# mLSTM projections as pairs in block products, with h as scratch, and the SWA groups and mLSTM heads in steps

## The chip, the cores and the metric

One core of one Trainium2 chip. The time is the device time of one execution in microseconds; a kernel's time is the median of its runs. Profiles come from one execution with the hardware profiler.

## The reference

Two layers on a residual stream h of 256 rows and 2048 columns, all in float32:

- Layer 0: RMSNorm, one input projection, then sliding-window attention (16 query heads of 64 in 4 groups, each group with one key and value head, window 128, ALiBi, a sink per head) beside an mLSTM with 4 heads (q and k of 128, v of 256, an output gate o, an input and a forget gate per head, chunks of 128 rows). Both results are joined and go through one output projection, which is added to h.
- Layer 1: RMSNorm, forgetting attention with 16 heads of 128, output projection, added to h.
- Behind each mixer: RMSNorm and a SwiGLU with 5632 hidden columns, added to h. At the end a last RMSNorm.

The change lies in the mixer of layer 0:

```python
proj = xn @ w_in
q_s, k_s, v_s, q_m, k_m, v_m, o_m, i_m, f_m = split_cols(proj, EVEN_SIZES)
attn = sliding_window_attention(q_s, k_s, v_s, sinks)
h = mlstm_chunkwise(q_m, k_m, v_m, i_pre, f_pre)
h = rms_norm(h, head_gain)
mem = sigmoid(o_m) * h
return concat([attn, mem]) @ w_out
```

## The kernel before

Every float32 matmul against weights is done as three float32r matmuls of 128 x 128 by 128 x 512: each operand is split into a high and a low part, and high by high, high by low and low by high are added in PSUM. Weights come in chunks of two k tiles by 512 columns (`load_raw`, on SyncE's DMA queue, four buffers). ScalarE rounds a chunk to `hi` (L153), VectorE subtracts to get `lo` (L154); `hi` and `lo` have six buffers. `gemm` (L167) runs a range of k tiles for both row tiles t: L181 to L183. `project` (L192) is a `gemm` over all 16 k tiles, 96 matmuls for 512 columns. x, transposed and split, lies in `xh` and `xl`; the mixer's result in `mh` and `ml`.

`pair_group` (L408) makes two projections of one x at once, for gate and up of the SwiGLU, for its down projection, and for q and k of layer 1. It goes through the eight pairs of k tiles in a given order. A plain pair costs 24 matmuls. In three of the eight pairs the two row tiles, two k tiles and two matrices are combined as in a fast matrix product: seven block products of three matmuls in place of eight, 21 matmuls. For it VectorE forms four differences of weight blocks (L439, L440, L444, L445), both engines split them (`split_plain`, L255 and L256), and beforehand the sums and differences of x are made for that pair (`sums_of`, `sums_from`). The products of the three pairs add up in four PSUM banks `prods`; at the end VectorE combines them into four tiles `c` (L464 to L468), and the plain part is added to them.

`Room` hands `pair_group` its buffers: the second matrix's raw chunks, `t4`, `c` and `tmp` from a pool, and the places for split differences, either from a pool or, in layer 1, in the free halves of `mh` and `ml`.

PSUM has two sets of four banks: `pa` (accumulators, tag acc) and `pm` (everything else: transposes `pp`, `ptm`, `ptv`, scores `p0`, `p1`, P times V `po`, gates `pu`, `pn`, `pb`, the heads' `pc` and `pom`).

Layer 0's mixer in the order of the code: keys and values of SWA (acc0), the first half of the SWA queries (acc1), while h is loaded and its squares are summed (L616, ScalarE); groups 0 and 1 of SWA; the second half of the queries; groups 2 and 3 (`swa`, `attention`); the tail of the output gate with the eight gate columns (264 columns); the chain of the gates: `pu`, two scans on VectorE (L725 to L733), `pn` (L739, L740), `pb` (L763), the decay matrix `dt_`; the rest of the output gate (512 and 256 columns, `gate_out`); q, its transposes; k, its transposes; q times k (`pq`); then, for each half of the value columns, a projection and two heads (`mlstm`). Then `close_layer` does the output projection (`out_proj`, L350) and the SwiGLU.

The order in which an engine runs its instructions is not that of the code: the framework lays it out when the kernel is built, by a timeline of its own, and puts ready matmuls of later projections into earlier gaps. Each engine runs its list in order. In the built order of the kernel before, the SWA groups stand among the matmuls of the output gate and of q, the heads among those of the values and of the output projection.

A head (L820) is: `pc`, copied to `ce`; per chunk of 128 rows `pom`, its denominator (ScalarE L832, VectorE L833, L836), `hv` (L837), its squares (ScalarE L839); a small power on GpSimd (L841); `hv` times the gate (L843); four transposes `ptv` (L854); split into `mh` and `ml`.

Of the kernel before, what the change touches and what calls it, by code (L numbers as in the profile page):

```python
# [7 lines left out]
F32 = mybir.dt.float32  # L8
# [34 lines left out]
V_AT = 8  # L43
MID = 6
# [12 lines left out]
def trunk(  # L57
# [158 lines left out]
    def sums_of(pool, sh, sl, copies, full=None):  # L216
        if full is None:
            full = pool.tile([P, 2, NT, P], F32, tag="tmp", name="full", bufs=2)
            copies(full.rearrange("p i t q -> p i (t q)"))
        s = pool.tile([P, 4, P], F32, tag="tmp", name="s4", bufs=2)  # L220
# [177 lines left out]

    def sums_from(room, sh, sl, lhs, pair):
# [6 lines left out]
        sums_of(room.pool, sh, sl, None, full)  # L406
# [64 lines left out]
    def ffn(layer, fp, sx, sd, key, idx_next=None, key_next=None, finish=None):  # L471
# [7 lines left out]
        for g0, g1 in zip(PARTS, PARTS[1:]):  # L479
# [4 lines left out]
            for g in range(g0, g1):  # L484
# [15 lines left out]
                if g == g1 - 1 and nk < 16:  # L500
                    for half in range(2):
                        pt = bank(par, "pf").rearrange("p (i q) -> p i q", i=2)
                        for i in range(2):
                            cs = (2 * half + i) * P
                            for t in range(NT):
                                nc.tensor.transpose(pt[:, i, t * P : (t + 1) * P], c[:, t, cs : cs + P], ident)
                        pair = 2 * (g - g0) + half
                        k = 2 * pair
                        split_plain(mh[:, k : k + 2, :], ml[:, k : k + 2, :], pt)
                        if pair in mixed_of(order):  # L510
                            j = mixed_of(order).index(pair)
                            sums_of(
                                fp, sd[0][:, j, :, :], sd[1][:, j, :, :], lambda full, pt=pt: nc.scalar.copy(full, pt)
                            )
                    continue
# [7 lines left out]
                def join(c=c, turned=turned, g=g, g0=g0, order=order):  # L523
# [8 lines left out]
                    for half in range(2):  # L532
                        pair = 2 * (g - g0) + half
                        if pair in mixed_of(order):
                            j = mixed_of(order).index(pair)
                            sums_of(
                                fp,
                                sd[0][:, j, :, :],
                                sd[1][:, j, :, :],
                                None,  # L540
                                ct[:, half * 512 : (half + 1) * 512].rearrange("p (i t q) -> p i t q", i=2, t=NT),
                            )
# [50 lines left out]
    def close_layer(layer, w_out, idx, key, begun=None, **rest):  # L593
        with tc.tile_pool(name=f"fp{layer}", bufs=2) as fp:
            nd = max(len(mixed_of(o)) for o in DOWN.values())
            sd = [fp.tile([P, nd, 4, P], F32R, name=f"sd{i}", bufs=1) for i in range(2)]
            out_proj(w_out, idx, key, (*sx, fp), begun)
            ffn(layer, fp, sx, sd, key, **rest)


# [17 lines left out]
    with tc.tile_pool(name="ev", bufs=1) as ev:  # L618
# [22 lines left out]
        with tc.tile_pool(name="sw", bufs=1) as sw:  # L641
# [17 lines left out]
            def swa(g, qn):  # L659
# [17 lines left out]
                for _ in attention(  # L677
# [10 lines left out]
                ):  # L688
# [15 lines left out]
        acc = project(wi, OFF_OM + 768, 256 + 8)  # L704
# [5 lines left out]
        gate_out(acc, 768, 256)  # L710
        nc.scalar.activation(gates, gates, AF.Tanh, scale=1.0 / CAP)
# [46 lines left out]
        with tc.tile_pool(name="mp", bufs=1) as mp:  # L758
            dt_ = mp.tile([P, ML_H, NT, P], F32, name="dt_")
# [18 lines left out]
            gate_out(project(wi, OFF_OM, NB), 0, NB)  # L778
            gate_out(project(wi, OFF_OM + NB, 256), NB, 256)
# [3 lines left out]
            qm = natural(mp, project(wi, OFF_QM, NB), NB, "qm", scale=rq)  # L783
# [7 lines left out]
            for g in range(0, ML_H, 2):  # L791
                transpose_many(
                    qmt[:, g : g + 2, :].rearrange("p g (t q) -> p (g t) q", q=P),
                    [qm[:, t, (g + i) * QK : (g + i + 1) * QK] for i in range(2) for t in range(NT)],
                )
            transpose_many(qst, [qsc[:, hh, :] for hh in range(ML_H)])
            km = natural(mp, project(wi, OFF_KM, NB), NB, "km")
            kmt = mp.tile([P, ML_H, S], F32, name="kmt")
            for g in range(0, ML_H, 2):
                transpose_many(  # L800
                    kmt[:, g : g + 2, :].rearrange("p g (t q) -> p (g t) q", q=P),
                    [km[:, t, (g + i) * QK : (g + i + 1) * QK] for i in range(2) for t in range(NT)],
                )
            kw = mp.tile([P, ML_H, QK], F32, name="kw")
            for hh in range(ML_H):
                nc.vector.tensor_scalar(
                    kw[:, hh, :], km[:, 0, hh * QK : (hh + 1) * QK], ex[:, 3, hh : hh + 1], None, op0=ALU.mult
                )
            for c in range(NT):
                pq = pm.tile([P, ML_H, P], F32, tag="pm", name="pq")  # L810
# [3 lines left out]
                nc.vector.tensor_tensor(out=dt_[:, :, c, :], in0=pq, in1=dt_[:, :, c, :], op=ALU.mult)  # L814

# [4 lines left out]
            def mlstm(hh):  # L820
                pc = pm.tile([P, NB], F32, tag="pm", name="pc")
                nc.tensor.matmul(pc[:, 0 : VD + 1], kw[:, hh, :], ve[:, 0, hh, :], start=True, stop=True)
                nc.vector.tensor_copy(ce[:, hh, :], pc[:, 0 : VD + 1])
                hv = mp.tile([P, NT, VD], F32, tag="hv", name="hv", bufs=2)
# [17 lines left out]
                for c in range(NT):  # L842
# [7 lines left out]
                    )  # L850
                pt = pm.tile([P, 2, S], F32, tag="pm", name="ptv")
# [6 lines left out]
            for g in range(2):  # L858
                acc = project(wi, OFF_VM + g * NB, NB)
                for t in range(NT):  # L860
                    nc.scalar.mul(
                        ve[:, t, 2 * g : 2 * g + 2, 0:VD],
                        acc[t].rearrange("p (h e) -> p h e", e=VD),
                        r[:, t : t + 1],
                    )
                mlstm(2 * g)
                mlstm(2 * g + 1)
# [3 lines left out]
    close_layer(0, w_out_even[0], 2, "f0", idx_next=1, key_next="m1")  # L871
# [4 lines left out]
    with tc.tile_pool(name="od", bufs=1) as od:  # L876
# [10 lines left out]
        for t in range(NT):  # L887
# [15 lines left out]
        halves = [  # L903
            [m[:, k : k + 4, :].rearrange("p (a b) s -> p a (b s)", a=2) for m in (mh, ml)] for k in (8, 12)
        ]
# [39 lines left out]
        for i in range(4):  # L945
# [14 lines left out]
            for m in range(2):  # L960
                for t in range(NT):
                    o = c[:, 2 * m + t, :]
                    nc.scalar.mul(o, o, r1[:, t : t + 1])
                    nc.vector.scalar_tensor_tensor(
                        out=o, in0=plain[m][t], scalar=r1[:, t : t + 1], in1=o, op0=ALU.mult, op1=ALU.add
                    )
# [126 lines left out]
```

## Time and profile before

| | |
|---|---|
| runs | 2119.54, 2118.51, 2115.81 us; median 2118.51 |
| profiled execution | 2117.76 us, its span 2116.1 us |
| granted clock of TensorE | 0.998 |
| share of the span: TensorE, VectorE, ScalarE, GpSimd | 99%, 84%, 60%, 2% |
| DMA | 420.96 MB, 199 GB/s |

How to read it: L12 is line 12 of the kernel before. PE is TensorE's matmuls, PEld its weight loads, DVE is VectorE, ACT ScalarE, POOL GpSimd, SP SyncE. A row of a timeline has the start in us from the span's start, the duration, engine, line, operation, what it writes and reads, and the shapes; in brackets the engine's idle time before it and what ended it. Matmuls overlap, so their durations are longer than the time from one to the next. A window's row has for each engine the busy time and the number of instructions, then the granted clock, the DMA engines' busy share and GB/s.

### The profile page before, as it was taken

How to read it: one execution, taken by the hardware profiler on the slowest of the kernel's cores; microseconds unless marked ns; L12 is line 12 of the kernel's file. 1: busy time of each engine (PE TensorE's matmuls, PEld its weight loads, DVE VectorE, ACT ScalarE, POOL GpSimd, SP SyncE). 2: the span in 40 equal slices, each digit the busy share in tenths (PEclk: the TensorE clock that was granted, in tenths of full speed). 3: DMA queues.
4: the chain of work that ended last, by engine and by line, in shares of the span. 5: the costliest groups of instructions: out<-in, count | busy, mean ns of one | idle time of the engine just before them, and what ended most of it. 6: DMA issues, size and time to landing. Idle time of an engine off the chain costs nothing.

```text
span 2116.1 us, 26910 instructions
## 1 busy us (share of the span) xinstructions
PE 2098.3 (99%) x9672; PEld 1742.4 (82%) x9672; DVE 1783.9 (84%) x2329; ACT 1272.5 (60%) x1623; POOL 49.2 (2%) x70
## 2 busy tenths in 40 slices
PE   8999999999999999999999999999999999999998
PEld 6888888888888888888888888888888888888886
DVE  6666567899999998999877878778999998998995
ACT  6565456665477646766565555566755667556763
POOL 2010000000000000000000000000000000000000
PEclk9999999999999999999999999999999999999999
DMA  9455556766677666775575655666656767657764
GB/s 310 145 170 144 170 193 194 217 201 198 200 219 218 210 201 209 228 219 185 177 221 177 179 169 165 206 198 198 215 182 220 221 209 207 221 189 209 229 200 139
DMA packets 258423, 420.96 MB, mean 199 GB/s; under 512 B 56512, under 2 KB 64752, under 8 KB 258288
## 3 DMA queue, kind: packets, MB, share of 16 engines
q1 hardware_dynamic: 256976, 415.49, 63.2%
q0 software_dynamic: 1168, 3.71, 0.6%
q8 instruction: 76, 1.25, 0.2%
q14 instruction: 59, 0.48, 0.1%
q10 hardware_dynamic: 144, 0.03, 0.0%
HBM read 406.57 MB, written 2.11 MB: 193 GB/s over the span
## 4 chain that ended last, share of the span: by engine, by line
PE 98%; DMA 1%; DVE 0%; issue 0%; ACT 0%; POOLq 0%; POOL 0%; SPq 0%; ACTq 0%
PE acc L366 19%; PE acc L367 19%; PE acc L368 19%; PE acc L183 7%; PE acc L181 7%; PE acc L182 7%; PE prod L367 5%; PE prod L368 5%; PE prod L366 5%; PE vacc L181 1%; PE vacc L183 1%; PE vacc L182 1%; PE ptm L267 1%; PE p L285 1%; PE po L337 1%; PE pt L233 0%
## 5 line engine op out<-in xcount | busy, mean ns | idle before, releaser
L153 ACT CAST hi<-raw 128x1024 fp32r<-128x1024 f32 (+2 forms) x670 | 682.8, 1032 | 515.5 <-PE acc L368 247.6
L154 DVE TENSOR_TENSOR lo<-raw,hi 128x1024 fp32r<-128x1024 f32 (+2 forms) x670 | 794.4, 1198 | 167.6 <-ACT hi L153 165.0
L367 PE MATMUL acc<-lo,xh 128*128 128x512 f32 x1121 | 436.6, 389 | 0.0
L366 PE MATMUL acc<-hi,xh 128*128 128x512 f32 x1121 | 433.0, 390 | 0.0
L368 PE MATMUL acc<-hi,xl 128*128 128x512 f32 x1121 | 431.5, 389 | 0.0
L366 PEld LDWEIGHTS acc<-hi,xh 128*128 128x128 f32 x1121 | 210.3, 188 | 44.3 <-DVE u L465 0.8
L368 PEld LDWEIGHTS acc<-hi,xl 128*128 128x128 f32 x1121 | 210.4, 188 | 43.7
L367 PEld LDWEIGHTS acc<-lo,xh 128*128 128x128 f32 x1121 | 210.4, 188 | 43.6
L367 PE MATMUL acc<-lo,mh 128*128 128x512 f32 x444 | 173.1, 390 | 0.0
L368 PE MATMUL acc<-hi,ml 128*128 128x512 f32 x444 | 171.1, 389 | 0.0
L366 PE MATMUL acc<-hi,mh 128*128 128x512 f32 x444 | 170.2, 389 | 0.0
L181 PE MATMUL acc<-hi,xh 128*128 128x512 f32 (+3 forms) x352 | 128.9, 370 | 7.7 <-ACT hi L153 7.1
L255 ACT CAST ht<-raw 128x1024 fp32r<-128x1024 f32 x94 | 98.7, 1050 | 55.3 <-issue 19.4
L183 PE MATMUL acc<-hi,xl 128*128 128x512 f32 (+3 forms) x352 | 129.6, 370 | 0.3 <-DVE xl L239 0.3
L182 PE MATMUL acc<-lo,xh 128*128 128x512 f32 (+3 forms) x352 | 129.8, 369 | 0.0
L181 PE MATMUL acc<-hi,mh 128*128 128x512 f32 x320 | 125.9, 394 | 1.2 <-ACT mh L255 1.2
L256 DVE TENSOR_TENSOR lt<-raw,ht 128x1024 fp32r<-128x1024 f32 x94 | 114.5, 1218 | 14.6 <-ACT ht L255 14.3
L182 PE MATMUL acc<-lo,mh 128*128 128x512 f32 x320 | 125.6, 393 | 0.0
L183 PE MATMUL acc<-hi,ml 128*128 128x512 f32 x320 | 123.5, 390 | 0.0
L255 ACT CAST ht<-t 128x1024 fp32r<-128x1024 f32 x94 | 98.8, 1051 | 38.4 <-PE prod L368 27.3
L256 DVE TENSOR_TENSOR lt<-t,ht 128x1024 fp32r<-128x1024 f32 x94 | 114.3, 1216 | 7.8 <-ACT ht L255 7.8
L255 ACT CAST hi<-raw 128x512 fp32r<-128x512 f32 (+1 forms) x109 | 68.8, 631 | 74.5 <-PE acc L368 63.5
(345 smaller groups left out, 3476.0 us busy)
## 6 DMA issues: line engine op xcount, KB each, us to landing
raw<-in_w_gate_dram SPq DMA_DIRECT2D x176, 512.0 KB, 4.6
raw<-in_w_up_dram SPq DMA_DIRECT2D x176, 512.0 KB, 4.7
raw<-in_w_down_dram SPq DMA_DIRECT2D x176, 512.0 KB, 4.9
raw<-in_w_in_odd_dram SPq DMA_DIRECT2D x88, 512.0 KB, 4.4
raw<-in_w_in_even_dram SPq DMA_DIRECT2D x64, 512.0 KB, 4.7
raw<-in_w_out_even_dram SPq DMA_DIRECT2D x32, 512.0 KB, 3.7
raw<-in_w_out_odd_dram SPq DMA_DIRECT2D x32, 512.0 KB, 4.6
raw<-in_w_in_odd_dram SPq DMA_DIRECT2D x8, 272.0 KB, 2.9
```

The lines of the kernel that those rows point to most:

```text
L153: latest[0] = nc.scalar.copy(hi[:, :, 0:n], raw[:, :, 0:n])
L154: nc.vector.tensor_tensor(out=lo[:, :, 0:n], in0=raw[:, :, 0:n], in1=hi[:, :, 0:n].bitcast(F32), op=ALU.subtract)
L181: nc.tensor.matmul(o, ah[:, ts], hi, start=(k == 0), stop=False)
L182: nc.tensor.matmul(o, ah[:, ts], lo, start=False, stop=False)
L183: nc.tensor.matmul(o, al[:, ts], hi, start=False, stop=(k == k_all - 1))
L255: nc.scalar.copy(dst_h, src)
L256: nc.vector.tensor_tensor(out=dst_l, in0=src, in1=dst_h.bitcast(F32), op=ALU.subtract)
L267: nc.tensor.transpose(pt[:, i, :], s_, ident)
L285: nc.tensor.matmul(p1[:, jj, :], q_of(j, 1), k_of(j), start=True, stop=True)
L366: nc.tensor.matmul(o, ah, hi, start=start, stop=False)
L367: nc.tensor.matmul(o, ah, lo, start=False, stop=False)
L368: nc.tensor.matmul(o, al, hi, start=False, stop=stop)
```

## The change

- q and k of the mLSTM are made by one `pair_group`, and both value halves by another, with three of eight pairs as block products each. Their sums of x are made once (`s0`).
- A class `Inside` (a `Room`) takes `c`, `t4` and `tmp` out of h, which is idle between the sums of its squares and the first addition into it. h is loaded a second time behind the values, by four DMAs on GpSimd's queue. The split differences lie in `mh` and `ml` from k tile 8 on (`free_halves`).
- `swa` and `mlstm` become generators. Groups 2 and 3 go on in steps between parts of two gate projections (264 and 256 columns); the 512 columns of the output gate come behind the q, k group, in parts between the transposes and `pq`. Transposes of q and k and `pq` use the `pa` banks.
- All four heads come behind the value group, in steps (`HEAD_STEPS`), with parts of the first two column blocks of the output projection between them (`begun0`, handed to `close_layer`).
- `fold`, used for q and k and by layer 1, scales and adds the plain part; for the values the same is written out into `ve`.

```diff
+HEAD_STEPS = ((0, 1), (0, 2), (1, 3), (0, 2), (1, 3), (2,), (3,))
...
+    class Inside(Room):
+        def t4(self):
+            return self.at[:, 1, 0 : 2 * NB].rearrange("p (a n) -> p a n", a=2)
+        def c(self):
+            return self.at[:, 0, :].rearrange("p (a n) -> p a n", a=4)
+        def tmp(self, shape, name):
+            self.turn = 1 - self.turn
+            v = self.at[:, 1, (2 + self.turn) * NB : (3 + self.turn) * NB]
...
-            for half in range(2):
-                qn = natural(sw, project(wi, OFF_QS + NB, NB) if half else acc1, NB, "qn")
-                swa(2 * half, qn)
-                swa(2 * half + 1, qn)
+            two, three_ = swa(2, qn), swa(3, qn)
+            tacc, oacc = new_acc(), new_acc()
+            gemm(tacc, x_of, wi, c_t, 264, 0, 2, KT)
+            next(two)
+            gemm(tacc, x_of, wi, c_t, 264, 2, 6, KT)
+            next(three_)
...
-            gate_out(project(wi, OFF_OM, NB), 0, NB)
-            gate_out(project(wi, OFF_OM + NB, 256), NB, 256)
+            halves = free_halves()
+            room = Inside(ev, 2, halves, h)
+            for j, pair in enumerate(mixed_of(QK_ORDER)):
+                sums_from(room, s0[0][:, j, :, :], s0[1][:, j, :, :], x_of, pair)
...
-            qm = natural(mp, project(wi, OFF_QM, NB), NB, "qm", scale=rq)
-            km = natural(mp, project(wi, OFF_KM, NB), NB, "km")
+            plain, c = pair_group(room, 0, x_of, sums_m, [(wi, OFF_QM), (wi, OFF_KM)], QK_ORDER)
+            fold(plain, c, (rq, r))
+            oacc = [bank(1, "oacc") for _ in range(NT)]
+            gemm(oacc, x_of, wi, OFF_OM, NB, 0, 6, KT)
...
-            for g in range(2):
-                acc = project(wi, OFF_VM + g * NB, NB)
...
-                mlstm(2 * g)
-                mlstm(2 * g + 1)
+            plain, c = pair_group(room, 0, x_of, sums_m, [(wi, OFF_VM), (wi, OFF_VM + NB)], QK_ORDER)
...
+            for n in range(4):
+                nc.gpsimd.dma_start(h[:, :, n * NB : (n + 1) * NB], xv[:, :, n * NB : (n + 1) * NB])
+            begun0 = [new_acc() for _ in range(2)]
+            fillers = [(m, k) for m in range(2) for k in range(0, 8, 2)]
+            heads = [mlstm(hh) for hh in range(ML_H)]
...
+            for step in HEAD_STEPS:
+                for hh in step:
+                    next(heads[hh], None)
+                fill_in(1)
...
-    close_layer(0, w_out_even[0], 2, "f0", idx_next=1, key_next="m1")
+    close_layer(0, w_out_even[0], 2, "f0", begun=begun0, idx_next=1, key_next="m1")
```

More of the change, by code (lines that the diff above doesn't have):

```diff
@@ L405, in sums_from @@
             )
-        sums_of(room.pool, sh, sl, None, full)
+        sums_of(room, sh, sl, None, full)
     def pair_group(room, par, lhs, sums, mats, order, todo=()):
@@ L596, in close_layer, with free_halves, fold @@
             sd = [fp.tile([P, nd, 4, P], F32R, name=f"sd{i}", bufs=1) for i in range(2)]
-            out_proj(w_out, idx, key, (*sx, fp), begun)
+            out_proj(w_out, idx, key, (*sx, Room(fp)), begun)
             ffn(layer, fp, sx, sd, key, **rest)
+    def free_halves():
+        return [[m[:, k : k + 4, :].rearrange("p (a b) s -> p a (b s)", a=2) for m in (mh, ml)] for k in (8, 12)]
+    def fold(plain, c, scales):
+        for m in range(2):
+            for t in range(NT):
+                o, f = c[:, 2 * m + t, :], scales[m][:, t : t + 1]
+                nc.scalar.mul(o, o, f)
+                nc.vector.scalar_tensor_tensor(out=o, in0=plain[m][t], scalar=f, in1=o, op0=ALU.mult, op1=ALU.add)
     acc0 = new_acc()
@@ L675, in half_of @@
                     return slice((j % 2) * HD, (j % 2 + 1) * HD)
-                for _ in attention(
+                yield from attention(
                     sw,
@@ L959, in trunk @@
             )
[L960 to L966, printed above, removed]
+            fold(plain, c, (r1, r1))
             if i < 3:
```

94 lines of the change are left out of this document (68 added, 26 removed).

## The prediction

> **What bounds the kernel now.** I read the page first: shares of busy time, then the chain of work that ended last, then the waits of TensorE.
>
> ```profile
> PE 2098.3 (99%) x9672; PEld 1742.4 (82%) x9672; DVE 1783.9 (84%) x2329; ACT 1272.5 (60%) x1623; POOL 49.2 (2%) x70
> ...
> PE 98%; DMA 1%; DVE 0%; issue 0%; ACT 0%; POOLq 0%; POOL 0%; SPq 0%; ACTq 0%
> ```
> ```profile
> PE acc L181 <- ACT hi L153: 7.1, 1, 7.1
> PE acc L181 <- ACT mh L255: 1.2, 1, 1.2
> ```
>
> TensorE (PE) is busy 99% and is 98% of the chain. Its waits in the whole execution are 7.1 us at the start, 1.2 us at one place, and crumbs. So the time is the sum of what TensorE issues, plus its few waits, and there is almost nothing to win but by issuing less. The profiled execution took 2117.76 us; the median of the runs is 2118.51, 0.75 more, so sums made on this execution read some 0.4 to 0.75 us low against the runs. A change within 0.2% (4.2 us) is about what a measurement of this kernel can't tell from none.
>
> What one matmul costs, and the 1.2 us wait, stand in the timeline of TensorE:
>
> ```profile
> 291.02 0.39 PE L182 MATMUL acc<-lo,mh 128*128 128x512 f32 x1
> 291.24 0.39 PE L183 MATMUL acc<-hi,ml 128*128 128x512 f32 x1
> 291.47 0.60 PE L854 MATMUL ptv<-ident,hv 128*128 128x128 f32 x4
> 293.25 0.50 PE L181 MATMUL acc<-hi,mh 128*128 128x512 f32 x1 [1.18 <-ACT mh L255]
> ```
>
> The column of 0.39 is a matmul from start to end; they overlap. From start to start there are 0.45 us for two (291.02 to 291.47), 0.225 each, and that is the price of a 512-wide matmul here. After the last head's transposes TensorE runs dry until ScalarE has converted that head into mh: 1.35 us from where the next matmul could have begun (291.90) to 293.25.
>
> The stage that changes lies between about 50 and 300 us:
>
> ```profile
> 50.00:300.00 250.00, 248.82 (x1299) 206.59 (x1298) 149.56 (x248) 130.66 (x231) 13.84 (x19) 0.99 0.55 165
> ```
>
> In order: TensorE, weight loads, VectorE, ScalarE, GpSimd, clock, DMA share, GB/s. VectorE is busy 150 of 250 us, ScalarE 131.
>
> **What the change takes away.** A projection costs 16 x 2 x 3 = 96 wide matmuls, four of them 384. As pairs, five plain steps are 24 matmuls each and three are 7 x 3 = 21, so a group has 183, and two groups 366. The built order of the changed kernel has 9482 matmul instructions against 9500: the 18 are really gone, and no transposes or small matmuls are added. 18 x 0.225 = -4.05 us. The 1.35 us go too: with all four heads behind the value group, its order puts 28 wide matmuls (6.3 us) ahead of the last head's transposes and 69 (15.5 us) behind them. Of these 69, 21 need no new head, so 4.7 us cover the two conversions that took 1.35. What is late next there is the heads' VectorE chain: ten splits (11.3 by the prices below), four folds (2.4) and, as an estimate, 3.5 us a head make some 28 us against 31 of TensorE, and the splits lie eight chunks ahead, so I put nothing on it. Together -5.4.
>
> **What it adds, off TensorE.** By the built order VectorE gets 24 differences, 9 splits, 8 combining steps and 8 folds of 512 columns more (49 x 0.60), six splits of 1024 (6.8), and 18 small operations for the sums of x (4.4), by the start-to-start times below: 41 us, in a stage where it has 100 us free: (150 + 41) / 250 = 76%. On the average it isn't the bound. It can be in one place: the q,k group starts while the last two SWA groups and the gates still run, and its plain steps serve as TensorE's filler. The prices there:
>
> ```profile
> 154.74 1.22 DVE L154 TENSOR_TENSOR lo<-raw,hi 128x1024 fp32r<-128x1024 f32 x1
> 155.87 0.69 DVE L286 SCALAR_TENSOR_TENSOR s<-p,bias 128x512 f32<-128x512 f32 x1
> 156.47 0.41 DVE L279 SCALAR_TENSOR_TENSOR s<-p,bias 128x256 f32<-128x256 f32 x1
> 156.80 0.68 DVE L286 SCALAR_TENSOR_TENSOR s<-p,bias 128x512 f32<-128x512 f32 x1
> 157.40 1.80 DVE L292 TENSOR_REDUCE mx<-s 128x4 f32<-128x512 f32 x2
> ...
> 164.37 0.17 DVE L314 TENSOR_TENSOR den<-den,es 128x8 f32<-128x8 f32 x1 [3.42 <-ACT es L313]
> 164.57 0.20 DVE L316 RECIPROCAL rec<-den 128x8 f32<-128x8 f32 x1
> 164.81 1.93 DVE L320 TENSOR_SCALAR s<-s,rec 128x128 f32<-128x128 f32 x8
> 166.66 1.21 DVE L154 TENSOR_TENSOR lo<-raw,hi 128x1024 fp32r<-128x1024 f32 x1
> ```
> ```profile
> 160.61 0.40 ACT L307 ACTIVATE s<-s,neg 128x128 f32<-128x128 f32 x1
> ...
> 164.14 0.19 ACT L313 ACTIVATE es<-es 128x8 f32<-128x8 f32 x1
> ```
> ```profile
> 153.58 0.71 PE L278 MATMUL p<-ks,qt 64*128 64x128 f32 x4
> ...
> 155.64 0.50 PE L183 MATMUL acc<-hi,xl 128*128 128x512 f32 x1
> ```
>
> Start to start VectorE takes 1.13 for a 1024-wide split, 0.60 for 512, 0.33 for 256, 1.73 for both reduces, 0.2 for a dependent tiny one, 1.85 for the eight scalings; ScalarE 3.53 for eight exponentials, TensorE 2.1 for one group's scores. A gate matmul of 256 columns I put at half a wide one, 0.11, and a transpose at 0.12, from the row at 291.47 (0.60 for four, the last one's own length in it).
>
> I walk this place along the changed order, zero at the end of the copy of group 2's transposed q. **VectorE** then has, up to group 3's row maxima: eight splits of 1024 (9.0), fifteen 512-wide (9.0), four 256-wide (1.3), reduces 0.6 + 1.13 + 1.73, three tiny (0.6): 23.4. **TensorE** has, up to group 2's probabilities: 75 wide matmuls (16.9), 25 narrow gate matmuls (2.8), two groups' scores (4.2), four transposes (0.5): 24.4. Group 2's exponentials start at 19.5 and end at 23.2, so VectorE's first scaled row is ready at 24.4, just as TensorE comes for it, and its eighth at 26.0. The twelve transposes (1.5 of work) end at 26.15: wait 0.25. TensorE's next matmul but one needs a split queued behind the scalings, ready at 27.25: wait 0.9. Five wide (28.4), then P times V of group 2, whose t0 copies stand behind group 3's exponentials on ScalarE (24.55 to 28.1; a copy of 512 columns, as VectorE's 0.60, to 28.7): wait 0.3. P times V takes 1.4, to 30.1 (half of the 2.74 that it took before together with the gates' first matmuls, 175.35 to 178.09 below); group 3's scalings end at 31.05, its transposes at 31.5; its own P times V and the gates' first matmuls end at 34.2. The rest is the gates' chain:
>
> ```profile
> 175.35 0.66 PE L337 MATMUL po<-t,vs 128*64 128x256 f32 x4
> ...
> 178.09 0.47 PE L182 MATMUL acc<-lo,xh 128*128 128x512 f32 x1
> 178.19 0.41 DVE L725 COPY ut<-pu 4x257 f32<-4x257 f32 x1
> ...
> 179.92 1.23 DVE L154 TENSOR_TENSOR lo<-raw,hi 128x1024 fp32r<-128x1024 f32 x1
> ...
> 183.53 0.38 PE L739 MATMUL pn<-ident,mt 4*128 4x4 f32 x2
> ...
> 184.84 1.97 PE L763 MATMUL pb<-mt,sel 4*128 4x256 f32 x8
> 186.74 0.95 PE L267 MATMUL ptm<-ident,qm 128*128 128x128 f32 x4
> ```
>
> Between pu and pn VectorE scans for 1.65 us. Before, TensorE had wide matmuls to run meanwhile (178.09 to 183.53); in the changed order only P times V of group 3 stands there, so 0.4 of waiting is open. pn (1.3) and pb (1.9) follow, to 37.7, and the wide matmuls resume. Waits by the walk 0.25 + 0.9 + 0.3 + 0.1 (the t0 copies of group 3) + 0.4 = 1.95; a dozen hand-overs that I took at zero may add 0.06 each, the size of the gaps in these rows: 0.7. So +2.6. If I take every duration in full (1.22, 0.69, 0.41, exponentials of 0.58 and 0.68 with their reads), VectorE's list is 26.2 and each exponential block 5.0, and the same walk gives waits of 8.5. The bounds are 0 and 8.5; I take 2.6, since the engines did overlap so in the rows.
>
> **The clock.** The windows of the trace at that place (columns as above):
>
> ```profile
> 183.55:186.96 3.41, 3.41 (x21) 2.86 (x21) 1.90 (x9) 0.46 (x2) 0.00 (x0) 1.00 0.76 228
> 186.96:190.37 3.41, 3.41 (x11) 2.83 (x10) 1.73 (x6) 3.24 (x9) 0.00 (x0) 0.50 0.04 13
> ```
>
> A window with only pn, pb and transposes is followed by one of the same length at clock 0.50; for some 3 us of it wide matmuls ran at half rate, which cost 1.5 us. In the changed order the stretch without a wide matmul grows from 3.8 us to 7.6 (30.1 to 37.7), so such a window comes again, probably a little dearer as it may reach into pb: 2.2 against 1.5, +0.7.
>
> [...]
>
> **The second load of x** is four DMAs of 512 KB on the GpSimd queue behind the value group's folding, and the heads' four small powers stand behind their issue. The first adds into h come some 45 us later. Nothing on TensorE: 0.
>
> Sum: 2117.76 - 5.4 + 2.6 + 0.7 = 2115.7, 0.13% under the median of the runs.
>
> **The rivals.** *VectorE bounds the SWA and gate stretch* (slower). The point is where the first scaled row comes, 24.4, as TensorE does: whatever VectorE and ScalarE lose from there, TensorE pays, and both groups' softmaxes pass through it. For it: the two queues are full without a gap there. Against it: before, VectorE stood idle 3.42 us waiting for the exponentials, so the stage has run looser than this. At its bound of 8.5, and one more slow window (1.7): 2117.76 - 5.4 + 8.5 + 0.7 + 1.7 = 2123.3. *Everything is covered*: no wait, and the slow window falls away as wide matmuls end up between (-1.5): 2110.9. [...] *The load of x collides* with the weights': 2.1 MB are 9.2 us at the 228 GB/s of the first row above, and four raw buffers of 12 matmuls each cover 10.8. Uncovered wholly: 2115.7 + 9.2 = 2124.9. That the block products save nothing isn't open, as the order has 18 fewer.
>
> **The numbers.** The walk's outcome 0.50, covered 0.15, VectorE-bound 0.20, clock 0.10, load 0.05. The walk's own range is 2112.5 to 2118.5, from waits between 0 and 5 us with the one slow window. Slower than the runs by over 0.2% means above 2122.7, faster means below 2114.3. Faster: 0.15 and two fifths of the walk's 0.50, 0.35. Slower: most of VectorE's 0.20 and of the load's 0.05, 0.23. Same: 0.42. The range that holds 8 in 10 is 2110.5 to 2123.0.
>
> **What would show it.** Right: 18 fewer matmuls; no wait on mh L255 near 292; waits under 1 us each between the last SWA scores and the first block product; one half-clock window right after pb. Wrong: waits of TensorE on VectorE's scalings or splits of several us there; several half-clock windows; or a wait for h or raw behind the heads.

## The result, and the profile after

The changed kernel takes 2114.57 us (median of 22 executions, 2112.12 to 2116.03) against 2118.06 us before (22 executions, 2115.44 to 2119.54): a ratio of 0.9984, 95% interval 0.9977 to 0.9990, so 3.5 us faster. The forecast was 2115.7 us. The profiled execution took 2115.51 us, with a span of 2113.8 against 2116.1 us before.

First the page of the changed kernel: busy time by engine, and the chain that ended last by engine.

```profile
PE 2096.8 (99%) x9654; PEld 1740.8 (82%) x9654; DVE 1823.7 (86%) x2402; ACT 1280.7 (61%) x1637; POOL 50.6 (2%) x74
...
PE 96%; DVE 2%; DMA 1%; issue 0%; ACT 0%; SPq 0%; DVEq 0%; POOLq 0%; POOL 0%; ACTq 0%
```

TensorE has 9654 matmuls against 9672. VectorE has 39.8 us more (1783.9 before). The chain now passes 2% through VectorE, where it was 0%. The view of TensorE's waits (us in total, times, longest) shows why:

```profile
PE acc L182 <- ACT hi L154: 6.6, 1, 6.6
PE acc L368 <- DVE lo L155: 0.5, 1, 0.5
PE acc L183 <- DVE lo L155: 0.3, 1, 0.3
```

The wait of 1.2 us for mh is gone. One of 0.5 us for a split on VectorE is new. In the timeline of TensorE the last head now runs straight on, and the new wait stands behind the transposes of group 2's probabilities. The split that it waits for stands behind the eight scalings in VectorE's order (last two rows):

```profile
280.32 0.60 PE L916 MATMUL ptv<-ident,hv 128*128 128x128 f32 x4
280.67 0.47 PE L183 MATMUL acc<-lo,mh 128*128 128x512 f32 x1
```
```profile
138.07 0.27 PE L334 MATMUL pp<-ident,s 128*128 128x128 f32 x1
138.86 0.50 PE L368 MATMUL acc<-lo,xh 128*128 128x512 f32 x1 [0.52 <-DVE lo L155]
```
```profile
135.67 1.93 DVE L321 TENSOR_SCALAR s<-s,rec 128x128 f32<-128x128 f32 x8
...
137.59 1.22 DVE L155 TENSOR_TENSOR lo<-raw,hi 128x1024 fp32r<-128x1024 f32 x1
```

The clock is the part that went otherwise. These are windows of 3.41 us behind that stretch (busy us of TensorE, weight loads, VectorE, ScalarE, GpSimd, then TensorE's granted clock):

```profile
145.57:148.99 3.42, 3.42 (x28) 2.86 (x25) 2.50 (x9) 1.10 (x2) 0.11 (x1) 1.00 0.00 0
148.99:152.40 3.41, 3.41 (x9) 2.29 (x8) 2.85 (x12) 1.38 (x5) 0.00 (x0) 0.50 0.00 0
152.40:155.81 3.41, 3.41 (x9) 2.64 (x9) 1.53 (x2) 2.56 (x6) 0.00 (x0) 0.50 0.00 0
```

There are two windows at half clock, where before had one (186.96 to 190.37 us). Only 9 matmuls fit into each; at the 0.227 us that a wide one takes at full clock some 15 do.

To add up where the 2.3 us between the two profiled spans come from, I took the start of every matmul to the start of the next, from 30 to 340 us, less what its shape takes in an undisturbed row (0.227 us for 512 columns, less for narrower ones). What is left over falls into half-clock windows, single waits, and many small hand-overs (the little that TensorE loses when it goes from one kind of matmul to another: the wide one at 280.67 above, the first behind transposes, takes 0.31 us to the next start, 0.08 more than in a row). A half-clock window costs 1.6 us; three executions of one and the same order show it, under e_after below. "Second" is the same kernel in a second profiled execution (run e_after below, span 2112.1 us).

| us, against before | forecast | first | second |
|---|---|---|---|
| 18 matmuls less | -4.05 | -4.1 | -4.1 |
| wait for mh at the last head | -1.35 | -1.35 | -1.35 |
| waits over 0.25 us in the stretch | +1.95 | +0.7 | +0.7 |
| hand-overs | +0.7 | +1.05 | +1.0 |
| half-clock windows | +0.7 | +1.6 | +0.05 |
| what is left (start, rest of the run) | 0 | -0.2 | -0.3 |
| span | -2.05 | -2.3 | -4.0 |

Between the two executions of one kernel lie 1.7 us, and the one half-clock window that the second has less accounts for 1.6 of them. The 22 executions' median lies between them.

The kernel before draws its windows too: its executions have mean granted clocks from 0.997 to 0.999. Grouped by that clock, the medians (99 executions of before, beside the experiments; 33 of the changed kernel; several chips) are these:

| mean granted clock | before, us (executions) | changed, us (executions) |
|---|---|---|
| 0.999 | 2116.1 (28) | 2112.3 (2) |
| 0.998 | 2117.9 (55) | 2113.9 (19) |
| 0.997 | 2119.1 (16) | 2115.3 (12) |

At an equal clock the change is worth 3.8 to 4.0 us. The changed kernel is at the lowest clock more often (12 of 33 against 16 of 99), which takes back some 0.5 us in the medians.

### The profile page after: what moved, and what is told of

It reads as the page before. It is cut to its first block, busy times and chain, and to the rows that moved or that the text cites. A ratio compares the mean times of both kernels' runs of the same rounds, so it can differ in the third digit from the quotient of the medians.

```text
span 2113.8 us, 26987 instructions
## 1 busy us (share of the span) xinstructions
PE 2096.8 (99%) x9654; PEld 1740.8 (82%) x9654; DVE 1823.7 (86%) x2402; ACT 1280.7 (61%) x1637; POOL 50.6 (2%) x74
## 3 DMA queue, kind: packets, MB, share of 16 engines
HBM read 408.67 MB, written 2.11 MB: 194 GB/s over the span
## 4 chain that ended last, share of the span: by engine, by line
PE 96%; DVE 2%; DMA 1%; issue 0%; ACT 0%; SPq 0%; DVEq 0%; POOLq 0%; POOL 0%; ACTq 0%
PE acc L367 20%; PE acc L368 20%; PE acc L369 20%; PE prod L367 5%; PE prod L368 5%; PE prod L369 5%; PE acc L184 5%; PE acc L183 5%; PE acc L182 5%; PE vacc L182 1%; PE vacc L184 1%; PE vacc L183 1%; DVE lo L155 1%; PE ptm L268 1%; PE po L338 1%
## 5 line engine op out<-in xcount | busy, mean ns | idle before, releaser
L154 ACT CAST hi<-raw 128x1024 fp32r<-128x1024 f32 (+1 forms) x664 | 676.9, 1031 | 486.9 <-PE acc L369 266.1
L155 DVE TENSOR_TENSOR lo<-raw,hi 128x1024 fp32r<-128x1024 f32 (+1 forms) x664 | 788.0, 1200 | 140.1 <-ACT hi L154 138.1
L368 PE MATMUL acc<-lo,xh 128*128 128x512 f32 x1207 | 470.2, 390 | 0.5 <-DVE lo L155 0.5
L367 PE MATMUL acc<-hi,xh 128*128 128x512 f32 x1207 | 466.6, 390 | 0.3 <-DVE u L488 0.2
L369 PE MATMUL acc<-hi,xl 128*128 128x512 f32 x1207 | 464.9, 389 | 0.0
L367 PEld LDWEIGHTS acc<-hi,xh 128*128 128x128 f32 x1207 | 226.6, 188 | 48.3 <-DVE u L488 1.1
L368 PEld LDWEIGHTS acc<-lo,xh 128*128 128x128 f32 x1207 | 226.6, 188 | 47.7 <-DVE lo L155 0.8
L257 DVE TENSOR_TENSOR lo<-raw,hi 128x512 fp32r<-128x512 f32 (+1 forms) x115 | 80.6, 701 | 24.6 <-ACT hi L256 24.5
L367 PEld LDWEIGHTS acc<-hi,mh 128*128 128x128 f32 x444 | 83.3, 188 | 17.5
L369 PEld LDWEIGHTS acc<-hi,ml 128*128 128x128 f32 x444 | 83.4, 188 | 17.3
```

Of the source, the lines that this page charges most:

```text
L154: latest[0] = nc.scalar.copy(hi[:, :, 0:n], raw[:, :, 0:n])
L155: nc.vector.tensor_tensor(out=lo[:, :, 0:n], in0=raw[:, :, 0:n], in1=hi[:, :, 0:n].bitcast(F32), op=ALU.subtract)
L257: nc.vector.tensor_tensor(out=dst_l, in0=src, in1=dst_h.bitcast(F32), op=ALU.subtract)
L367: nc.tensor.matmul(o, ah, hi, start=start, stop=False)
L368: nc.tensor.matmul(o, ah, lo, start=False, stop=False)
L369: nc.tensor.matmul(o, al, hi, start=False, stop=stop)
```

## The experiments

Each run was timed in eleven executions against 33 of the kernel before on the same chip. The table gives the medians' difference from before; the intervals reach about 1.9 us to each side, so differences under 1 us between two rows are not resolved, and one of 1 to 2 us needs the traces beside it.

| run | us | against before | ratio, 95% interval |
|---|---|---|---|
| e_plain | 2118.15 | +0.5 | 1.0003, 0.9995 to 1.0012 |
| e_plain_q | 2116.89 | -0.7 | 0.9997, 0.9989 to 1.0006 |
| e_plain_v | 2115.64 | -2.0 | 0.9992, 0.9983 to 1.0001 |
| e_vbefore | 2117.44 | -0.2 | 0.9999, 0.9990 to 1.0008 |
| e_spread | 2113.49 | -4.0 | 0.9981, 0.9973 to 0.9990 |
| e_best_spread | 2114.43 | -3.1 | 0.9987, 0.9978 to 0.9996 |
| e_vload_q | 2118.13 | +0.6 | 1.0003, 0.9994 to 1.0012 |
| e_noreload | 2113.80 | -3.7 | 0.9982, 0.9973 to 0.9990 |
| e_after | 2114.50 | -3.4 | 0.9982, 0.9973 to 0.9991 |
| e_spread_o4 | 2113.85 | -4.0 | 0.9982, 0.9973 to 0.9991 |
| e_vload_q4 | 2118.33 | +0.5 | 1.0002, 0.9993 to 1.0011 |
| e_vload_v | 2113.88 | -4.0 | 0.9982, 0.9973 to 0.9991 |

**Parts of the change undone: does the saving of the block products arrive?** Three runs keep the new order of the work and multiply all eight k pairs plainly: in both groups, in q and k alone, in the values alone.

```diff
# e_plain_q; e_plain_v does the same to the value group, e_plain both
-            plain, c = pair_group(room, 0, x_of, sums_m, [(wi, OFF_QM), (wi, OFF_KM)], QK_ORDER)
-            fold(plain, c, (rq, r))
+            plain, c = plain_group(room, [(wi, OFF_QM), (wi, OFF_KM)])
+            for m in range(2):
+                for t in range(NT):
+                    nc.scalar.mul(c[:, 2 * m + t, :], plain[m][t], (rq, r)[m][:, t : t + 1])
```

> Both groups (q,k and the two value blocks) go through all eight pairs as plain pairs, 192 matmuls each, with everything else of the changed kernel kept; the sums of x are not made. Theory (the 18 matmuls are worth 0.225 us each, but the block products of q,k cost cover in the SWA and gate stretch): against the changed kernel +4.05 for the matmuls, -1.0 for TensorE's waits in the stretch, -1.7 to -2.3 for one of its two half-clock windows, so about +1 (0 to +2), that is some 2.5 us faster than the kernel before. Rival (the saving comes in full and the stretch has nothing to do with the block products): +4, that is about 0.5 us slower than before, with the two half-clock windows still there.

> Only q,k go as plain pairs (192 matmuls); the value blocks keep their block products. Theory: +2.0 for nine matmuls, -1.0 for the waits, -1.7 to -2.3 for a half-clock window: -1 against the changed kernel, some 4.5 us faster than before. Rival: +2.0, some 1.5 us faster than before.

> Only the value blocks go as plain pairs; q,k keep their block products. Theory and rival agree here on the matmuls, +2.0 against the changed kernel (some 1.5 us faster than before); the theory says besides that the waits and the two half-clock windows of the SWA and gate stretch stay as they are.

My theory here was that the q and k block products give back in waits and clock a good part of what they save. It fell. With both groups plain the kernel is 0.5 us slower than before and so 4.0 us slower than the changed one (0.5 and 3.5 against their own runs of before): 18 matmuls at 0.227 us are 4.1. The saving arrives, whole as far as the medians resolve it. With one group in blocks the result lies between (-0.7 and -2.0), as nine matmuls each should give, within the intervals. The profiled run with q and k plain shows that the half-clock windows don't come from the block products of q and k:

```profile
161.34:164.76 3.42, 3.42 (x19) 2.62 (x19) 2.41 (x10) 1.24 (x3) 0.00 (x0) 1.00 0.70 178
164.76:168.17 3.41, 3.41 (x9) 2.28 (x8) 1.90 (x3) 2.56 (x8) 0.00 (x0) 0.50 0.34 129
168.17:171.58 3.41, 3.41 (x9) 2.64 (x9) 1.23 (x1) 1.04 (x1) 0.00 (x0) 0.50 0.00 0
```

Two windows again, behind pn and pb, and here the stretch before them is short. What the q and k blocks do cost is the one wait on lo (0.7 us from start to start), which is absent from this run's waits.

The run with everything plain shows what the rest of the change, the steps and the moved heads, is worth alone: the wait for mh gone (-1.35) and hand-overs of 1.1 us more in the profiled run. That leaves about nothing, and 0.5 us slower was measured, which is not resolved from nothing.

**The values and heads as before.** The value blocks as two plain projections, each followed by its two heads; q and k stay in blocks.

```diff
-            plain, c = pair_group(room, 0, x_of, sums_m, [(wi, OFF_VM), (wi, OFF_VM + NB)], QK_ORDER)
...
+            for g in range(2):
+                acc = project(wi, OFF_VM + g * NB, NB)
...
+                mlstm(2 * g)
+                mlstm(2 * g + 1)
```

> The value blocks and the heads as in the kernel before (two projections, two heads behind each, no steps, no part of the output projection begun between them); q,k with block products and the SWA steps as in the changed kernel; x is loaded again behind q,k. Theory: +2.0 for nine matmuls and +1.35 for the wait on mh at the last head, which comes back: +3.4 against the changed kernel, equal to before. Rival (the order of the heads gives nothing): +2.0 and no wait on mh.

Measured 0.2 us under before, as expected. The wait at the last head is back, in the timeline of TensorE:

```profile
291.07 0.60 PE L914 MATMUL ptv<-ident,hv 128*128 128x128 f32 x4
292.85 0.50 PE L182 MATMUL acc<-hi,mh 128*128 128x512 f32 x1 [1.18 <-ACT mh L256]
```

It has as many matmuls as the run with plain values, which has no such wait and is 1.8 us faster; as a difference of medians that is barely resolved, and the trace has 1.35 of it in this one wait. So the move of the heads, and not the block products, takes it away.

**The run of four-row matmuls spread out.** The four pb matmuls go behind the q and k group, among the following projection.

```diff
-            for g in range(2):
-                pb = pm.tile([P, 2, NT, P], F32, tag="pm", name="pb")
...
-            gemm(oacc, x_of, wi, OFF_OM, NB, 0, 6, KT)
+            for hh in range(ML_H):
+                nc.tensor.matmul(pb[:, i, :, :]..., sel[:, hh, :], mt, start=True, stop=True)
...
+                if hh < 3:
+                    gemm(oacc, x_of, wi, OFF_OM, NB, 2 * hh, 2 * hh + 2, KT)
```

> The four pb matmuls (eight records, 3.4 us of four-row work in one run) stand in the changed kernel behind 13 po, pu and pn matmuls, where two half-clock windows follow (excess over full clock 3.9 us in its profiled run). Here they are moved behind the q and k group and put two by two among the 512-wide matmuls of the following gemm. Theory (the run of four-row matmuls calls the half clock): no half-clock window between 100 and 300 us, granted clock .999 in most executions, 1.5 to 3 us faster than the changed kernel, so 4.7 to 6 us faster than before, about 2112.3. Rival (any stretch without 512-wide matmuls calls it): a window stays behind the po and pn matmuls, within 0.7 us of the changed kernel, about 3.3 faster than before.

The windows of its profiled run, around the same po and pn matmuls:

```profile
141.45:144.86 3.41, 3.33 (x28) 2.48 (x29) 2.27 (x6) 1.58 (x3) 0.00 (x0) 1.00 0.03 9
144.86:148.27 3.41, 3.41 (x24) 2.47 (x24) 2.50 (x8) 1.96 (x4) 0.11 (x1) 1.00 0.00 0
148.27:151.69 3.42, 3.42 (x19) 2.92 (x19) 3.42 (x11) 1.60 (x4) 0.00 (x0) 1.00 0.19 29
```

No half-clock window is left between the first 13 us and the last few. (At both ends the profiles of before and of the changed kernel are slow as well: up to 12.9 and 12.5 us a 512-wide matmul takes 0.43 us from start to start, and the last 4.0 and 5.6 us are at clock 0.50.) A window of transposes, P times V, pu and pn without one wide matmul (the first row) calls none; so the first theory holds for the cause. Its size did not: 4.0 us faster than before, 0.6 us under the changed kernel and not the 1.5 to 3 expected. The 3.9 us that the expectation puts on two windows are too high; two cost 3.2 (under e_after below). Some 0.9 us are given back in hand-overs: over the same matmuls, from 30 us to 340, the profiled run is only 0.7 us shorter than e_after's, though one window of 1.6 is gone. And the changed kernel itself has fewer such windows in the mean than its first profiled execution showed.

**The gate chain earlier as well, and plain pairs first.** The gate chain is emitted as soon as its accumulator is full (not in the lines shown), and the q and k group starts with four plain pairs.

```diff
+            first = ((0, 0), (0, 1), (0, 4), (0, 5), (1, 2), (1, 3), (1, 6), (0, 7))
-            plain, c = pair_group(room, 0, x_of, sums_m, [(wi, OFF_QM), (wi, OFF_KM)], QK_ORDER)
+            plain, c = pair_group(room, 0, x_of, sums_m, [(wi, OFF_QM), (wi, OFF_KM)], first)
```

> As the run before, and the gate chain is issued as soon as its accumulator is full, among the remaining SWA work, and the q and k group begins with four plain pairs, so that the lo split of the first block product is not waited for. Theory: the wait of 0.7 us at 138 us goes as well; 0.5 to 1 us faster than the kernel with pb spread alone, about 2111.6, 5.5 to 7 us faster than before. Rival (the waits only move to the next consumer): the same as the kernel with pb spread alone, within 0.4 us.

> The kernel with pb spread, and in the q and k group four plain pairs ahead of the first block product instead of two. VectorE is busy without a gap from 118 to 138 us in the changed kernel, and the split that the tensor engine waits for there (0.7 us) stands at the end of that queue. Theory (the first block products stand too close behind the SWA work on VectorE): with two more plain pairs ahead the wait of 0.7 us goes and the po waits with it, no half-clock window; 0.5 to 1 us faster than with pb spread alone, 4.5 to 5 us faster than before. Rival (VectorE's queue is only made late elsewhere, at the end of the group, where a split of the o block stands behind the fold): a wait of 0.5 to 0.8 us near 169 us instead, the same as with pb spread alone.

The second of them has pb spread and the new order of pairs alone. In both the wait at 138 us is gone, and in both another stands near 169 us: 0.8 us, for a split of the output gate's weights in the one, for mh of a block product in the other. The rival was right about the waits: VectorE's work is only late elsewhere. The second run's time is that of pb spread alone, as the rival said. In the first the hand-overs grew by another 1.3 us, and its median is 0.9 us above the kernel with pb spread alone, where the theory had 0.5 to 1 us less and the rival at most 0.4 more; nine of the eleven executions with pb spread alone lie below this run's lowest, so some loss is likely. All eleven executions of both had a mean granted clock of 0.999; of the changed kernel's eleven beside the second, nine had 0.998, one 0.999 and one 0.997. The clock is steadier, and little of that reaches the median.

**How much slack VectorE has.** The first two of the four differences of each block-product pair are done three times: some 7 us of VectorE work more in one group (twelve operations at 0.60 us).

```diff
-            nc.vector.tensor_tensor(out=t4[:, 0, :], in0=rb[:, 0, :], in1=ra[:, 0, :], op=ALU.subtract)
-            nc.vector.tensor_tensor(out=t4[:, 1, :], in0=rb[:, 1, :], in1=rb[:, 0, :], op=ALU.subtract)
+            for _ in range(again):  # 3 in one group, 1 elsewhere
+                nc.vector.tensor_tensor(out=t4[:, 0, :], in0=rb[:, 0, :], in1=ra[:, 0, :], op=ALU.subtract)
+                nc.vector.tensor_tensor(out=t4[:, 1, :], in0=rb[:, 1, :], in1=rb[:, 0, :], op=ALU.subtract)
```

> The changed kernel with the two differences of each block product in the q and k group done three times instead of once: about 2.4 us of VectorE work more for each of three block products, 7 us in all. Theory (VectorE paces only the first block product there, by a wait of 0.7 us; the rest has cover): 0 to 2.5 us slower than the changed kernel, VectorE busy up by about 7 us. Rival (VectorE is the bound of the q and k stretch, as one rival of the prediction said): most of the 7 us arrives, 5 to 7 us slower than the changed kernel.

> The changed kernel with the differences of each block product of the value group done three times: 7 us of VectorE work more there. Theory (VectorE is idle for a fifth of that stretch and stands ahead of the tensor engine): within 1 us of the changed kernel. Rival (VectorE bounds every block product): 4 to 5 us slower, as in the q and k group.

> The run before with the differences of each q and k block product done three times, 2.4 us of VectorE work more for each, 7 us in all; the same load cost 4 to 5 us where two plain pairs stood ahead. Theory (VectorE has no slack next to the SWA work, and some behind it): at most 2 us slower than the run before. Rival (the whole q and k group is bound by VectorE): 4 us or more slower, as with the group as changed.

In the value group the 7 us cost nothing (0.6 us under e_after, not resolved). In the q and k group 4.0 of them arrived (+0.6 against -3.4). My theory of 0 to 2.5 fell there; the rival's 5 to 7 was too much. The changed kernel's own windows at that place show how near it stands (first the changed kernel, then the run with q and k plain):

```profile
118.00:135.00 17.00, 17.00 (x83) 13.32 (x82) 17.00 (x27) 9.67 (x23) 0.38 (x1) 1.00 0.47 136
```
```profile
118.00:135.00 17.00, 17.00 (x85) 13.56 (x84) 13.03 (x27) 10.16 (x23) 0.00 (x0) 1.00 0.46 142
```

VectorE, the third busy time in a row, is busy in 17.00 of 17.00 us with the block products and in 13.03 without. TensorE is still busy in all of them, since it has plain products to do meanwhile. With the load tripled it runs out of them just behind:

```profile
118.00:135.00 17.00, 17.00 (x83) 13.51 (x83) 17.00 (x28) 9.14 (x18) 0.05 (x1) 1.00 0.42 125
135.00:150.00 15.00, 10.85 (x77) 7.70 (x77) 12.31 (x37) 8.91 (x31) 0.00 (x0) 1.00 0.22 71
```

TensorE's waits there are for splits of a weight chunk and for the copy of a group's transposed probabilities:

```profile
PE po L338 <- ACT t L331: 1.6, 1, 1.6
PE acc L368 <- DVE lo L155: 1.2, 1, 1.2
PE acc L367 <- ACT hi L154: 1.1, 1, 1.1
```

The third run puts four plain pairs ahead of the first block product and has the same load. It was to cost at most 2 us there and cost 4.5 (+0.5 against -4.0), so two more plain pairs ahead on TensorE do not give VectorE slack. Its timelines say why. VectorE:

```profile
139.06 0.16 DVE L298 TENSOR_TENSOR mx<-mx,sink 128x8 f32<-128x8 f32 x1
139.14 1.92 DVE L321 TENSOR_SCALAR s<-s,rec 128x128 f32<-128x128 f32 x8
140.97 0.68 DVE L257 TENSOR_TENSOR lo<-raw,hi 128x512 fp32r<-128x512 f32 x1
141.58 0.68 DVE L468 TENSOR_TENSOR raw<-raw,h 128x512 f32<-128x512 f32 x1
142.18 1.22 DVE L257 TENSOR_TENSOR ml<-raw,mh 128x1024 fp32r<-128x1024 f32 x1
143.31 0.17 DVE L299 TENSOR_SCALAR neg<-mx 128x8 f32<-128x8 f32 x1
```

and behind it ScalarE, then TensorE:

```profile
143.51 0.41 ACT L308 ACTIVATE s<-s,neg 128x128 f32<-128x128 f32 x1 [3.48 <-DVE neg L299]
...
147.04 1.04 ACT L331 COPY t<-pp 128x512 f32<-128x512 f32 x2
```
```profile
147.65 0.86 PE L338 MATMUL po<-t,vs 128*64 128x256 f32 x4 [2.17 <-ACT t L331]
```

The row maxima of group 3 are complete at 139.2 us. The tiny operation behind them, the negated maximum of 0.17 us, follows at 143.3, because group 2's scalings and three operations of a block product stand between in VectorE's order. ScalarE waits 3.5 us for it; the exponentials come late; a copy of transposed probabilities stands behind them on ScalarE, and TensorE waits 2.2 us for that copy. In the run with the same order of pairs and without the load (e_spread_o4) the negated maximum stands 5.6 us earlier, ScalarE waits 1.6 us for it and TensorE does not wait there:

```profile
137.70 0.17 DVE L299 TENSOR_SCALAR neg<-mx 128x8 f32<-128x8 f32 x1
```

So in this run the load is paid mainly through the softmax that shares the queue, and little through the block product's own operands (a wait of 0.8 us for a split at 174 us, where e_spread_o4 has one of 0.6 at 170). In the run with two plain pairs ahead it is paid both ways, as its waits above show. In the traces of before and of the changed kernel VectorE runs its 2329 and 2402 operations in the built order, line by line, and so does ScalarE its 1496 and 1513 (table loads and accumulator reads aside).

The wait costs this profiled execution a second time. The window in which TensorE stands idle is followed by a half-clock one, though pb is spread here:

```profile
144.57:147.99 3.42, 1.25 (x8) 0.66 (x9) 1.31 (x4) 3.42 (x15) 0.00 (x0) 1.00 0.78 240
147.99:151.40 3.41, 3.41 (x22) 2.58 (x19) 3.04 (x12) 1.30 (x4) 0.00 (x0) 0.50 0.17 64
```

Whether its other executions have that window isn't known; five of the eleven have a mean granted clock of 0.999 and are no faster (2117.5 to 2118.8 us).

**The second load of x left out.**

```diff
-            for n in range(4):
-                nc.gpsimd.dma_start(h[:, :, n * NB : (n + 1) * NB], xv[:, :, n * NB : (n + 1) * NB])
```

> The changed kernel without the second load of x into h; h then holds scratch where the residual adds x, so the residual is left out of the computation. Theory (the load of 4 MB is hidden, nobody waits for it): within 0.4 us of the changed kernel, about 3.4 faster than before. Rival (it collides with the weight stream): 1 to 3 us faster than the changed kernel.

3.7 us faster than before against 3.4 to 3.5 with the load: nothing that can be measured. (That kernel leaves the residual out. The load is 2.1 MB, not the 4 of the expectation: the core read 406.57 MB against 408.67.) In the changed kernel's profile no engine waits for h, and the load's rows are these (GpSimd's group):

```profile
L934 POOL DMA_DIRECT2D h<-in_x_dram x4 | 3.0, 750 | 39.1 <-DMA raw<-in_w_out_even_dram 37.1 <-DVE ve L925 2.0
```

**The changed kernel once more**, beside e_spread_o4, e_vload_q4 and e_vload_v on the same chip, unedited.

> The changed kernel once more, unedited, beside the three others of this call on one chip. Every theory expects 3.4 us faster than before, and one or two half-clock windows near 150 us in the profiled run.

It came out 3.4 us faster than before, with one half-clock window, which follows the one that holds pb:

```profile
146.43:149.84 3.41, 3.41 (x21) 2.77 (x20) 2.57 (x10) 1.24 (x3) 0.11 (x1) 1.00 0.00 0
149.84:153.25 3.41, 3.41 (x9) 2.64 (x10) 2.06 (x8) 2.31 (x7) 0.00 (x0) 0.50 0.00 0
```

The run with the value group's load has the same order of matmuls in this stretch, and its profiled execution has no such window:

```profile
144.56:147.98 3.42, 3.42 (x32) 2.89 (x31) 2.18 (x6) 1.10 (x2) 0.11 (x1) 1.00 0.00 0
147.98:151.39 3.41, 3.41 (x16) 2.65 (x16) 3.30 (x14) 1.53 (x6) 0.00 (x0) 1.00 0.00 0
```

Here the boundary of two windows cut pb differently: the last po and pn in the first with a little of pb, and the rest of pb together with the first wide matmuls in the second.

From the first pu to the thirteenth wide matmul behind pb the changed kernel and these two runs have one and the same order, with two windows, one and none. The first pu starts at 143.91, 143.76 and 143.82 us, and that wide matmul here:

```profile
155.92 0.39 PE L367 MATMUL acc<-hi,xh 128*128 128x512 f32 x1
```
```profile
154.19 0.40 PE L367 MATMUL acc<-hi,xh 128*128 128x512 f32 x1
```
```profile
152.66 0.39 PE L367 MATMUL acc<-hi,xh 128*128 128x512 f32 x1
```

That is 12.01, 10.43 and 8.84 us: 1.6 us for each half-clock window.

Of all versions e_spread has the lowest median, 2113.49 us, 4.0 us under before. It is surely faster than before, and against the changed kernel (3.4 to 3.5) its lead is not resolved: e_vload_v, which only adds work to the changed kernel, came out 4.0 under before as well.

## Why the prediction came out right

- **The 18 matmuls, -4.05.** Right in count and in size: 4.0 us between both groups plain and the change.
- **The wait for mh, -1.35.** Right, and with the reason given: the run with the values and heads as before has the wait back, and its median is 1.8 us above the run with plain values.
- **VectorE's added work, 41 us.** 39.8 measured. The step "on the average it isn't the bound" was sound but hid how near it came: in the 17 us from 118 us on, where the first block products are made, VectorE has no idle time, 7 us more of work there cost 4.0, and 7 us more in the value group cost nothing. The rival of VectorE as the bound named the right place, and the chain through the softmaxes that it named is part of the price (2.2 us of waiting in e_vload_q4, 1.6 in e_vload_q); the change as built stays just short of it.
- **The walk of that stretch, +2.6.** The sum was too high. The 0.9 us for a split behind the scalings measured 0.7 (from 138.07 to 138.86 less one transpose) and stands at the matmul that the walk named. The 0.3 for P times V measured 0.24. The others, 0.25, 0.1 and 0.4, did not show as waits. So the waits, put at 1.95, measured 0.7. Hand-overs, put at 0.7, measured 1.0. Together 1.7.
- **The clock, +0.7.** A half-clock window came again, as forecast, but its number is a draw: profiled executions of this stretch show none, one and two, which cost 0, 1.6 and 3.2 us, and before's one window is a draw as well. None shows three or more, so the 0.10 for a dearer clock has no run behind it. Against before the term was +1.6 in the first profiled execution and +0.05 in the second; by the table of clocks it is some +0.5 in the medians. The prediction had named several half-clock windows as a sign of being wrong, and the first execution has two. Its reason was wrong in part: it counted the whole stretch without a wide matmul, transposes included. Windows of transposes, P times V, pu and pn alone kept the full clock in every profiled execution; the run of pb calls the half clock.
- **The second load of x, 0.** Right, as far as the medians resolve it.

So the mechanism was right in the main: fewer matmuls, the covered wait, and little lost on VectorE. Two terms were mis-sized. The walk was too dear by 0.9 us, and the clock too cheap by 0.9 in the first profiled execution, so the forecast span comes within 0.25 us of that one by luck. In the medians the errors do not cancel, and the walk's 0.9 is most of the 1.1 us by which the forecast lies above the measured 2114.57. The total is no proof of the single terms; the runs above are.

## What to carry to other kernels

When work moves from a saturated engine to one with "room on the average", look at the windows right where it lands and at what else shares that queue: 17.00 of 17.00 us here stood beside 76% for the stage, and the next 7 us cost 4. A short operation on which another engine's chain depends had better not stand behind long ones in its engine's order (in e_vload_q4 the negated maximum of 0.17 us ran 4.1 us behind the row maxima, and ScalarE stood 3.5 us for it); no run here moved it ahead, so what that would win is not shown. And a half-clock window is a draw: one and the same order of matmuls had none, one and two, which is 3.2 us between the first and the last. So compare several profiled executions before an effect of 2 us is put down to an edit.

## What the runs showed of the hardware

Ten of the fourteen profiled executions have half-clock windows in this stretch. TensorE is busy all through the window ahead of the first of them (3.41 of 3.41 us) in nine, so busy time doesn't tell when the clock will halve. In these nine that window held five to eight of the eight pb records (four rows each) and at most six wide matmuls. The case with the most wide ones is e_vload_q, with six; e_vbefore has five of them beside all of pb:

```profile
147.74:151.15 3.41, 3.41 (x17) 2.73 (x18) 3.33 (x12) 1.44 (x6) 0.00 (x0) 1.00 0.00 0
151.15:154.57 3.42, 3.42 (x9) 2.66 (x9) 2.53 (x5) 3.26 (x9) 0.00 (x0) 0.50 0.00 0
```

Seven pb records with seven wide matmuls called none (e_vload_v), nor did pb split in pairs among wide ones. Windows of some 25 to 30 records of transposes, P times V, pu and pn, with no pb and at most two wide matmuls, kept the full clock afterwards, all fifteen of them. A second half-clock window followed where the first still held two or three pb records (the changed kernel's first execution and e_plain_q), and not where it held wide matmuls alone. The tenth case is e_vload_q4, where TensorE stood idle for 2.2 us of the window; 1.6 us of idling in e_vload_q called none. In the trace of the changed kernel the clock goes to half at 148.99 us, back at 155.81 and to half again at 2108.24: the 6.827 us at half clock are two windows of 3.413, and the 1952.42 us behind them 572 of the same length. In the executions with none, one and two the first window edge behind the first pu came 0.7, 2.7 and 1.7 us after its start (144.56, 146.43 and 145.57 us); why it falls where it does is not shown. What else calls the half clock than the run of pb (e_spread) and 2.2 us of idling (e_vload_q4), these runs bound but don't settle.
